# A fourteenth slot in the big SBUF pool of a hybrid attention and gated delta rule step

## The chip, the cores and the metric

The kernel runs on one core of a Trainium2 chip, as one program and one launch. The metric is the device time of an execution in microseconds (us). Engines are named as in the profile: PE is TensorE's matmuls and PEld its weight loads, DVE is VectorE, ACT is ScalarE, POOL is GpSimd, SP is SyncE.

## The reference, cut to what matters

One layer of a decoder is run on a prompt of 256 tokens and on 8 sequences that each add one token to a past of 2048. Two mixers run side by side on one normalised input: sparse attention (compressed, selected and window branches) and a gated delta rule (a short causal convolution on q, k and v, then chunks of 64 tokens that carry a state of 128 x 128 per head). All arithmetic is in 32-bit floats.

```python
def decoder_layer(x_p, x_s, cache_cmp, cache_slc, st_win, st_S, st_conv, page_table, w):
    ...
    (q_a, kvc, kvs, kvw, g_nsa, z_a, qkv_b, a_b, b_b, z_b, gate_a, gate_b) = split_proj(rms_norm(x_p, norm_w) @ w_in)
    q, kvc, kvs, kvw = nsa_project(q_a, kvc, kvs, kvw, q_norm_w, k_norm_slc_w, k_norm_win_w)
    o_cmp, o_slc, o_win = nsa_prompt(q, kvc, kvs, kvw, cw, slopes)
    y_a = nsa_merge(o_cmp, o_slc, o_win, g_nsa, z_a, w_pa)
    y_b, S_p, conv_p = gdn_branch(qkv_b, a_b, b_b, z_b, zero_conv, zero_S, *gw)
    y_p = merge_residual(x_p, y_a, y_b, gate_a, gate_b, w_o)
    ...
def gdn_branch(qkv, a, b, z, conv_buf, S0, conv_w, a_log, dt_bias, gdn_norm_w, w_pb):
    buf = jnp.concatenate([conv_buf.astype(qkv.dtype), qkv], axis=1)
    c = jax.nn.silu(causal_conv(buf, conv_w)).astype(jnp.float32)
    ...
    o, S = gdn_chunked(q, k, v, g, beta, S0.astype(jnp.float32))
    ...
    return o @ w_pb, S.astype(S0.dtype), buf[:, -(CONV_W - 1):]
```

The outputs are the new rows of both inputs, the rows for all caches, the window buffers, and the states of the delta rule and of the convolution. `gdn_chunked` solves one triangular system of 64 x 64 per head and chunk.

## The kernel before, in words

**Matmuls.** Prompt and decode rows lie side by side as 264 columns (`TT`, 256 + 8). Each product of 32-bit matrices is made of three faster ones: a weight is split into `hi` (rounded, by ACT, L332) and `lo` (the rest, by DVE, L333), the input likewise into `xh` and `xl`, and `three` (its matmuls run through the helper line L205) adds `xh` x `hi`, `xl` x `hi` and `xh` x `lo` in PSUM. A unit of 1024 x 128 weights is a *half*: 8 blocks, 24 matmuls of 264 columns.

**The loop.** The list `halves` holds all halves in the order of the projections (`ORDER`, L30): first those of the compress stage (`CQ`: pages of the cache are loaded by `load_pages`, L386, by SP and POOL in turn, split at L409 and L410, and multiplied with `w1h` and `w1l`), then the projections of q, k, v and the gates, the two output projections, and the last one. For half i the loop loads the weights of half i + 4 (SP, L327), splits those of half i + 2, and issues the matmuls of half i in two parts. After each part `tick()` lets every running generator issue its next piece: `g_xnorm` (normalises the input; its squares are summed by the DVE reduction `xa`, L295), the attention's, `g_gdn` (prompt part of the delta rule), `g_gdn_dec` (its decode part, from L1361).

**Order.** SP's and POOL's instructions run in the order in which the program writes them. The order on PE, DVE and ACT is set at build time by a scheduler that simulates the engines, so a change of buffers can shift it.

**The big pool.** `slot()` takes a tile of 8448 B per partition from the pool `s8`, with `NS` = 13 buffers. Tiles take them in turn as they come free: cache pages, the input (`xt`), the split weights of the compress stage, q/k/v rows (`qkvr`), the tile `qm` (masked decode queries), the state tiles `sst`, the tiles of the delta rule (`At`, `U`, `prod`), and others. A tile that takes a used buffer waits for its last reader.

**The delta rule's prompt part.** POOL writes the diagonal 16 x 16 blocks of `At` to memory (`ad`, L1190) and reads them back one per lane into `prod` (L1197); DVE inverts them there in 15 steps (L1205, L1206), POOL scatters the inverses into `U` through memory (`td`, L1210 to L1216), and PE builds the inverse of the whole from them (`inv`).

**Its decode part.** Four state tiles `sst`, each for two sequences, are loaded by ACT (L1370), read by PE (`sw`), scaled (ACT, L1459) and added to (DVE, L1460), and stored by ACT (`o_Ss`, L1463); after each store the load of the tile after next is issued from the same queue. Before that, the old convolution rows `cd` (loaded by SP at L1058, 2304 B per partition) are written on to the output by POOL (L1374) and used by DVE (L1383). The decode temporaries `dsq`, `dx`, `dr`, `deb`, `wq`, `dod` and `dvn` are tiles of their own in the pool `tp`.

**The scratch.** The program reserves 8192 B for POOL's dynamic transfers (`dynamic_dma_scratch_size`, in `build`).

Of the kernel before, what the change touches and what calls it, by code (L numbers as in the profile page):

```python
# [20 lines left out]
NB = 8  # L21
# [123 lines left out]
def program(tc, A):  # L145
# [6 lines left out]
        ctxs.append(p)  # L152
        return p.__enter__()

    NS = 13
    cp = pool("cp")
    st = pool("st")
    s8 = pool("s8", bufs=NS)
# [10 lines left out]
    def slot(name, shape, dt=F32):  # L169
        return s8.tile(shape, dt, tag="s8", name=name)  # L170
# [68 lines left out]
    gd = cp.tile([128, 64], F32, name="gd")  # L239
    grow = cp.tile([128, 2], F32, name="grow")  # L240
    acc2 = cp.tile([128, 128], F32, name="acc2")
    cd = cp.tile([128, 24, 3, NB], F32, name="cd")
    cpo = cp.tile([128, 24, 3], F32, name="cpo")
    qss = cp.tile([128, 2, 8], F32, name="qss")
    beh = cp.tile([128, 2, 8], F32, name="beh")
# [255 lines left out]
    def g_qstat(h):  # L501
        yield
        pt = psb("qtr")
        jk = tp.tile([128, 128], F32, name="jk", tag="jk")
        for t in range(2):
            tr(pt[:, 128 * t:128 * t + 128], L["qT"][:, h, 128 * t:128 * t + 128])
        for t in range(2):
            S.activation(jk, pt[:, 128 * t:128 * t + 128], AF.Square, accum_out=ssq[:, t, h:h + 1])
        if h == 7:
            yield  # L510
            rsq(rqs, ssq, 1.0 / 128, EPS, [128, 2, 8])
            sl = C("slp").rearrange("p (t h) -> p t h", t=2)
            V.tensor_scalar(srq, ssq, 1.0 / 128, EPS, ALU.mult, ALU.add)
            V.tensor_mul(srq, srq, rqs)
            V.tensor_mul(srq, srq, sl)
            V.tensor_scalar(rqs, rqs, SCALE, None, ALU.mult)
            qr = L["qT"][:, :, TP:TT]
            sq = tp.tile([128, 8, NB], F32, name="qsq", tag="qsq")
            S.activation(sq, qr, AF.Square)
            yield 2  # L520
            p2 = psb("qss")
            mm(p2[:, 0:64], ones, sq.rearrange("p h b -> p (h b)"))
            rd = tp.tile([128, 64], F32, name="qrd", tag="qrd")
            rsq(rd, p2[:, 0:64], 1.0 / 128, EPS, [128, 64])
            o = qd.rearrange("p g b r -> p g r b")
            for g in range(2):
                V.scalar_tensor_tensor(o[:, g], qr[:, 4 * g:4 * g + 4, :], P("qw"),
                                       rd.rearrange("p (g r b) -> p g r b", g=2, r=4)[:, g], ALU.mult, ALU.mult)
            qx = slot("qm", [128, 640])
            G.memset(qx, 0.0)  # L530
            L["qdp"] = qdp = qx[:, 0:128]
            L["qm"] = qm = qx[:, 128:640].rearrange("p (j i c) -> p j i c", j=4, i=4)
            for bp in range(2):
                V.tensor_copy(qdp[:, 64 * bp:64 * bp + 64].rearrange("p (g c) -> p g c", g=2)[:, :, 0:16]
                              .rearrange("p g (i r) -> p g i r", r=4),
                              qd.rearrange("p g (i c) r -> p c g i r", c=2)[:, bp])
            for i in range(4):
                V.tensor_copy(qm[:, :, i, 4 * i:4 * i + 4],
                              qdp.rearrange("p (j c) -> p j c", j=4)[:, :, 4 * i:4 * i + 4])
            mark("q")  # L540
# [511 lines left out]
    def ev_qkv(j):  # L1052
        def f(ps):
            k, h = j // 8, j % 8
            if h == 0:
                L["qkv", k] = slot("qkvr", [128, 8, TT])
                if k == 0:
                    SP.dma_start(cd, A["cst8"])  # L1058
                if k == 1:
                    L["ktk"] = slot("ktk", [128, 2, 8, 128])  # L1060
                if k == 2:
                    L["vbt"] = slot("vbt", [128, 2, 8, 128])
# [301 lines left out]
    def g_gdn_dec():  # L1364
# [6 lines left out]

        state(0)
        state(2)
        G.dma_start(A["o_convs"][:, :, 0:2, :], cd[:, :, 1:3, :])  # L1374
        cw = P("cw").rearrange("p (j i) -> p j i", i=4)
        cv = tp.tile([128, 24, NB], F32, name="dcv", tag="a", bufs=NA)
# [8 lines left out]
        mark("gnew")  # L1385
        S.activation(th, cv, AF.Tanh, scale=0.5)
        V.scalar_tensor_tensor(cv, th, 1.0, cv, ALU.add, ALU.mult)
        sq = tp.tile([128, 16, NB], F32, name="dsq", tag="dsq", bufs=2)
        S.activation(sq, cv[:, 0:16], AF.Square)
        x = tp.tile([72, 2, 64], F32, name="dx", tag="dsq", bufs=2)  # L1390
        V.memset(x, 0.0)
        eg8 = tp.tile([128, NB], F32, name="eg8", tag="eg8")
        S.activation(eg8[32:40], sm[32:40, TP:TT], AF.Exp)
# [6 lines left out]
        pt = PGD("dg")  # L1400
        mm(pt[:, 0:128], ones, sq.rearrange("p h b -> p (h b)"))
        mm(pt[:, 128:256], ones[0:72, :], x.rearrange("p a c -> p (a c)"))
        r = tp.tile([128, 128], F32, name="dr", tag="dsq", bufs=2)
        rsq(r, pt[:, 0:128], 1.0, 4 * EPS, [128, 128])
        eb = tp.tile([128, 2, 64], F32, name="deb", tag="deb")
        S.activation(eb, pt[:, 128:256].rearrange("p (a c) -> p a c", a=2), AF.Copy)
        f64 = lambda a: a.rearrange("p h b -> p (h b)")
        qk = cv[:, 0:16]
        V.scalar_tensor_tensor(f64(cv[:, 0:8]), f64(cv[:, 0:8]), SCALE, r[:, 0:64], ALU.mult, ALU.mult)
        V.tensor_mul(f64(cv[:, 8:16]), f64(cv[:, 8:16]), r[:, 64:128])  # L1410
        q, k, v = f64(cv[:, 0:8]), f64(cv[:, 8:16]), f64(cv[:, 16:24])
        wq = tp.tile([128, 80, 2], F32, name="wq", tag="wq")
        V.memset(wq[:, 64:80], 0.0)
        u = tp.tile([128, 64], F32, name="du", tag="dcp")
        kq = tp.tile([128, 64], F32, name="dkq", tag="qsq")
# [6 lines left out]
        p2 = PGD("dq")  # L1422
        mm(p2[:, 0:64], ones, kq)
        V.tensor_copy(kq, p2[:, 0:64])
        od = tp.tile([128, 64], F32, name="dod", tag="dod")
        vn = tp.tile([128, 64], F32, name="dvn", tag="dvn")
        hb3 = lambda a: a.rearrange("p (h b) -> p h b", h=8)
        yield 2
        for b0 in range(0, NB, 2):
# [270 lines left out]


def build(m):
    nc = _bacc.Bacc("TRN2", target_bir_lowering=False, num_devices=1, dynamic_dma_scratch_size=8192)
    A = {}
    for k, a in m.items():
        A[k] = nc.dram_tensor(k, a.shape, mybir.dt.from_np(a.dtype), kind="ExternalInput").ap()
# [35 lines left out]
```

## Time and profile before

| what | value |
|---|---|
| median of 3 runs | 1135.54 us (1135.36 to 1137.25) |
| the profiled execution | 1137.88 us |
| its span, first to last instruction | 1136.2 us |
| its mean granted clock of TensorE | 0.994 of full speed |
| PE busy | 1112.4 us, 98% of the span, 9558 matmuls |
| PEld busy | 1069.3 us, 94% |
| DVE busy | 697.1 us, 61% |
| ACT busy | 572.7 us, 50% |
| POOL busy | 144.2 us, 13% |
| DMA | 222.17 MB, 196 GB/s in the mean |

The busy shares are means over the whole execution. Matmuls are pipelined and their ends are modelled, so PE's spacing, from the start of one matmul to the start of the next, says more than its busy time. Idle time of an engine that is not the bottleneck costs nothing. What one profiled execution shows is compared with its own time, 1137.88 us, and only then with the median.

### The profile page before, as it was taken

Reading aid. Unit: us, or ns where it says so; the run is one execution under the profiler, and the core shown is the slowest. Engines: PE = TensorE matmul, PEld = TensorE weight load, DVE = VectorE, ACT = ScalarE, POOL = GpSimd, SP = SyncE. Lnnn points to the kernel's source line nnn. Section 1 sums busy time; section 2 is a strip of 40 time slices with the busy share of each in tenths; the row PEclk is TensorE's granted clock in tenths of the full one; section 3 lists DMA queues with packets and bytes.
Section 4 is the critical chain, followed back from the end, with each engine's and each line's share of the span. In section 5 each row is a group of like instructions: output and inputs, shape, how many; then the busy total and the mean of one; then the engine's idle time right before and its main releaser. Section 6 shows DMA issues by size and latency. Waiting matters only on the chain.

```text
span 1136.2 us, 25323 instructions
## 1 busy us (share of the span) xinstructions
PE 1112.4 (98%) x9558; PEld 1069.3 (94%) x9558; DVE 697.1 (61%) x1523; ACT 572.7 (50%) x1138; POOL 144.2 (13%) x227
## 2 busy tenths in 40 slices
PE   4999999999999999999999999999999999999998
PEld 3989999999999987897989999999999999999998
DVE  3578565443657776783566577677547575487443
ACT  4445655444634766673454465545344554444332
POOL 4430244200001310113022100102000000000000
PEclk9989999999999999999999899999999999999999
DMA  9873676435445784568998755657454355556663
GB/s 302 255 241 124 202 205 203 152 95 160 161 138 177 218 214 135 159 196 220 281 390 291 268 174 176 201 179 220 138 187 148 119 165 177 181 184 223 201 236 125
DMA packets 77069, 222.17 MB, mean 196 GB/s; under 512 B 10625, under 2 KB 27850, under 8 KB 75410
## 3 DMA queue, kind: packets, MB, share of 16 engines
q1 hardware_dynamic: 59346, 164.36, 44.7%
q0 software_dynamic: 15008, 44.98, 13.8%
q10 hardware_dynamic: 2592, 11.21, 2.6%
q8 instruction: 75, 1.23, 0.4%
q14 instruction: 48, 0.39, 0.1%
HBM read 202.90 MB, written 17.60 MB: 194 GB/s over the span
## 4 chain that ended last, share of the span: by engine, by line
PE 92%; DVE 1%; ACT 0%; issue 0%; ACTq 0%
PE acc L205 77%; PE inv L205 1%; PE po L205 1%; PE gtr L202 1%; PE pvo L205 1%; PE ps L205 1%; PE gsc L205 1%; PE cf L205 1%; PE kk L205 1%; PE vnb L202 1%; PE uw L205 1%; DVE xt L306 1%; PE pst L202 0%; PE og L205 0%; PE wsc L205 0%; PE kvtr L202 0%
## 5 line engine op out<-in xcount | busy, mean ns | idle before, releaser
L333 DVE TENSOR_TENSOR lo<-raw,hi 128x1024 fp32r<-128x1024 f32 (+1 forms) x250 | 304.8, 1220 | 212.5 <-ACT hi L332 206.1
L205 PE MATMUL acc<-xh,hi 128*128 128x264 f32 (+1 forms) x1488 | 433.8, 292 | 0.0
L332 ACT ACTIVATE hi<-raw 128x1024 fp32r<-128x1024 f32 (+1 forms) x250 | 263.9, 1056 | 329.7 <-PE acc L205 269.0
L205 PE MATMUL acc<-xl,hi 128*128 128x264 f32 (+1 forms) x1488 | 426.9, 287 | 0.5 <-issue 0.5
L205 PE MATMUL acc<-xh,lo 128*128 128x264 f32 (+1 forms) x1488 | 426.3, 287 | 0.0
L205 PEld LDWEIGHTS acc<-xh,hi 128*128 128x128 f32 (+1 forms) x1488 | 281.0, 189 | 7.6 <-issue 7.0
L205 PEld LDWEIGHTS acc<-xh,lo 128*128 128x128 f32 (+1 forms) x1488 | 280.0, 188 | 2.7 <-issue 2.2
L205 PEld LDWEIGHTS acc<-xl,hi 128*128 128x128 f32 (+1 forms) x1488 | 281.1, 189 | 1.5 <-issue 1.0
L205 PE MATMUL acc<-hi,w1h 128*128 128x254 f32 (+1 forms) x512 | 148.1, 290 | 15.9 <-ACT hi L409 15.9
L205 PE MATMUL acc<-lo,w1h 128*128 128x254 f32 (+1 forms) x512 | 147.4, 288 | 3.4 <-DVE lo L410 3.2
L205 PE MATMUL acc<-hi,w1l 128*128 128x254 f32 (+1 forms) x512 | 145.7, 285 | 0.0
L410 DVE TENSOR_TENSOR lo<-rawc,hi 128x512 fp32r<-128x512 f32 (+2 forms) x136 | 84.0, 656 | 52.5 <-ACT hi L409 48.1
L205 PEld LDWEIGHTS acc<-hi,w1h 128*128 128x128 f32 x512 | 98.4, 192 | 16.0 <-ACT hi L409 15.9
L409 ACT ACTIVATE hi<-rawc 128x512 fp32r<-128x512 f32 (+2 forms) x136 | 74.7, 599 | 62.7 <-PE acc L205 58.0
L205 PEld LDWEIGHTS acc<-lo,w1h 128*128 128x128 f32 x512 | 99.2, 194 | 4.8 <-DVE lo L410 4.5
L205 PEld LDWEIGHTS acc<-hi,w1l 128*128 128x128 f32 x512 | 99.0, 193 | 0.1
L386 POOL DMA_DIRECT2D rawc<-ccmp x125 | 67.3, 538 | 98.2 <-issue 72.3
L205 PE MATMUL acc<-oh,hi 128*128 128x264 f32 x256 | 73.5, 287 | 0.0
L205 PE MATMUL acc<-oh,lo 128*128 128x264 f32 x256 | 72.9, 285 | 0.0
L205 PE MATMUL acc<-ol,hi 128*128 128x264 f32 x256 | 72.7, 284 | 0.0
L205 PE MATMUL acc<-mh,hi 128*128 128x264 f32 x256 | 72.6, 284 | 0.0
L205 PE MATMUL acc<-ml,hi 128*128 128x264 f32 x256 | 72.5, 283 | 0.0
(452 smaller groups left out, 1476.4 us busy)
## 6 DMA issues: line engine op xcount, KB each, us to landing
raw<-win SPq DMA_DIRECT2D x184, 512.0 KB, 3.5
raw<-wpab SPq DMA_DIRECT2D x32, 512.0 KB, 3.9
raw<-wo SPq DMA_DIRECT2D x32, 512.0 KB, 4.3
rawc<-ccmp SPq DMA_DIRECT2D x126, 128.0 KB, 2.7
rawc<-ccmp POOLq DMA_DIRECT2D x125, 128.0 KB, 3.3
raw<-w SPq DMA_DIRECT2D x8, 512.0 KB, 7.6
wk<-winK SPq DMA_DIRECT2D x8, 512.0 KB, 11.1
o_wk<-wk POOLq DMA_DIRECT2D x8, 512.0 KB, 9.0
```

The lines of the kernel that those rows point to most:

```text
L202: T.transpose(out, in_, ident[0:n, 0:n])
L205: T.matmul(out, lhsT, rhs, start=start, stop=stop, **k)
L306: V.scalar_tensor_tensor(xt[i][:, k, :], xt[i][:, k, :], P("nw")[:, kk:kk + 1], rx, ALU.mult, ALU.mult)
L332: S.activation(self.hi, self.raw, AF.Copy)
L333: V.tensor_sub(self.lo, self.raw, self.hi)
L386: e.dma_start(rawc[kv, b][j // 8][:, j % 8].rearrange("p s c g -> p (s c g)"), src[kv, bass.ds(r, 1)].rearrange("o d f -> (o d) f"))
L409: S.activation(h, src, AF.Copy)
L410: V.tensor_sub(l, src, h)
```

## The change

`NS` goes from 13 to 14, and the room for the 8448 B of the new slot is made in three places:

- The convolution rows `cd` are no longer a tile of their own. They take columns 640 to 1216 of `qm`, whose tile grows from 640 to 1216 columns in the slot it has anyway. POOL still clears only the first 640.
- The seven decode temporaries become parts of two tiles `za` and `zb` of 384 columns, of the tag `zz`, which the softmax of the attention uses (2 buffers).
- The scratch for dynamic transfers is halved, from 8192 to 4096 B.

```diff
-    NS = 13
+    NS = 14
...
-    cd = cp.tile([128, 24, 3, NB], F32, name="cd")
...
-            qx = slot("qm", [128, 640])
-            G.memset(qx, 0.0)
+            qx = slot("qm", [128, 1216])
+            G.memset(qx[:, 0:640], 0.0)
+            L["cd"] = qx[:, 640:1216].rearrange("p (j i b) -> p j i b", j=24, i=3)
...
-                    SP.dma_start(cd, A["cst8"])
+                    SP.dma_start(L["cd"], A["cst8"])
...
         state(0)
         state(2)
+        za, zb = (tp.tile([128, 384], F32, name=n, tag="zz", bufs=2) for n in ("dga", "dgb"))
+        cd = L.pop("cd")
...
-        sq = tp.tile([128, 16, NB], F32, name="dsq", tag="dsq", bufs=2)
+        sq = zb[:, 0:128].rearrange("p (h b) -> p h b", b=NB)
...
-        x = tp.tile([72, 2, 64], F32, name="dx", tag="dsq", bufs=2)
+        x = zb[0:72, 128:256].rearrange("p (a c) -> p a c", a=2)
...
-        r = tp.tile([128, 128], F32, name="dr", tag="dsq", bufs=2)
+        r = zb[:, 0:128]
...
-        eb = tp.tile([128, 2, 64], F32, name="deb", tag="deb")
+        eb = za[:, 0:128].rearrange("p (a c) -> p a c", a=2)
...
-        wq = tp.tile([128, 80, 2], F32, name="wq", tag="wq")
+        wq = za[:, 128:288].rearrange("p (c w) -> p c w", w=2)
...
-        od = tp.tile([128, 64], F32, name="dod", tag="dod")
-        vn = tp.tile([128, 64], F32, name="dvn", tag="dvn")
+        od, vn = za[:, 288:352], zb[:, 256:320]
...
-    nc = _bacc.Bacc("TRN2", target_bir_lowering=False, num_devices=1, dynamic_dma_scratch_size=8192)
+    nc = _bacc.Bacc("TRN2", target_bir_lowering=False, num_devices=1, dynamic_dma_scratch_size=4096)
```

Source lines behind L526 move by one or two. SP and POOL keep their order. On PE, DVE and ACT the scheduler arranges some instructions in another way; three places follow.

DVE where the inversion of the 16 x 16 blocks begins (`zt` and `ol` belong to the gated attention output, `lo` to a weight of the projections, `prod` to the inversion). Before:

```order
L1490 SCALAR_TENSOR_TENSOR zt<-zt,acc 128x264
L1491 SCALAR_TENSOR_TENSOR zt<-zt,qT 128x264
L1198 MEMSET prod 128x256
L1201 MEMSET prod 128x512
L1199 MEMSET prod 128x16
L333 TENSOR_TENSOR lo<-raw,hi 128x1024
L1493 TENSOR_TENSOR ol<-zt,oh 128x264
L1205 TENSOR_TENSOR prod<-prod 128x1
```

And in the change:

```order
L1494 TENSOR_TENSOR ol<-zt,oh 128x264
L332 TENSOR_TENSOR lo<-raw,hi 128x1024
L1491 SCALAR_TENSOR_TENSOR zt<-zt,acc 128x264
L1492 SCALAR_TENSOR_TENSOR zt<-zt,qT 128x264
L1205 TENSOR_TENSOR prod<-prod 128x1
L1206 TENSOR_REDUCE prod<-prod 128x1
L1205 TENSOR_TENSOR prod<-prod 128x4
```

The first step of the inversion stands behind a `zt` three units of the output gate earlier, the one that ran at 738.43 us before, and the clearing of `prod` has moved further ahead.

ACT around the second store of a state tile, with what each entry waits for (`DMA..` is a transfer's landing, `hi` a weight's split, `gate` a sigmoid of the output gates; the scaling factor is `deb` before and `dga` in the change). Before:

```order
L332 ACTIVATE hi<-raw 128x1024 [waits DMAHW1_49,DVE_49,PE_49]
L1504 ACTIVATE gate<-acc 128x264 [waits PE_49]
L1463 DMA o_Ss<-sst 128x2048 [waits DVE_49]
L332 ACTIVATE hi<-raw 128x1024 [waits DMAHW2_49,PE_49,Activation_49]
L1459 ACTIVATE sst<-sst,deb 128x128 [waits PE_49] x5
```

And in the change:

```order
L1464 DMA o_Ss<-sst 128x2048 [waits DVE_49]
L331 ACTIVATE hi<-raw 128x1024 [waits DMAHW1_49,PE_49,Activation_49]
L1505 ACTIVATE gate<-acc 128x264 [waits PE_49]
L331 ACTIVATE hi<-raw 128x1024 [waits DMAHW2_49,PE_49,Activation_49]
L1460 ACTIVATE sst<-sst,dga 128x128 [waits PE_49] x6
L1370 DMA sst<-stS 128x2048 [waits DMAHW3_49]
L1460 ACTIVATE sst<-sst,dga 128x128 [waits PE_49]
```

The load of the fourth state tile now stands five entries behind the store and waits for its landing. Before, that load came much later, at 839.1 us.

PE at the first matmuls of the inverse. Before they stand in a half of the gates' projections, which multiplies `xh` and `xl`:

```order
L205 MATMUL acc<-xh,hi 128x264
L205 MATMUL acc<-xl,hi 128x264
L205 MATMUL inv<-U,At 128x64 x8
L205 MATMUL acc<-xh,lo 128x264
L205 MATMUL acc<-xh,hi 128x264
```

In the change they stand in the last matmuls of a half of the first output projection, which multiplies `oh` and `ol`:

```order
L205 MATMUL acc<-oh,hi 128x264
L205 MATMUL acc<-ol,hi 128x264
L205 MATMUL acc<-oh,lo 128x264
L205 MATMUL acc<-oh,hi 128x264
L205 MATMUL inv<-U,At 128x64 x8
L205 MATMUL acc<-ol,hi 128x264
L205 MATMUL acc<-oh,lo 128x264
L205 MATMUL acc<-xh,hi 128x264
```

The inverse has moved by 162 entries of PE's order towards the start, about 20 us of matmuls, and stays among them.

## Rows read from the trace of the kernel before

**Rows 1.** The page, busy time, share of the span and instructions.

```profile
PE 1112.4 (98%) x9558; PEld 1069.3 (94%) x9558; DVE 697.1 (61%) x1523; ACT 572.7 (50%) x1138; POOL 144.2 (13%) x227
```

**Rows 2.** What PE waited for: us in total, times, longest (us).

```profile
PE acc L205 <- ACT hi L409: 15.9, 1, 15.9
PE acc L205 <- DVE lo L410: 3.2, 2, 2.6
...
PE acc L205 <- issue: 0.5, 1, 0.5
```

**Rows 3.** The chain that ended last: start (us), length (us), what.

```profile
537.64 3.01 PE acc L205 x24
...
705.76 5.80 PE acc L205 x48
```

**Rows 4.** Timeline of DVE: start, us, what, [idle before, releaser].

```profile
67.20 4.14 DVE L295 TENSOR_REDUCE xa<-xsq 128x264 f32<-128x2112 f32 x1 [0.85 <-ACT xsq L294]
```

**Rows 5.** Windows: us, PE, PEld, DVE, ACT, POOL busy (instructions), PEclk, DMA, GB/s.

```profile
72.00:76.00 4.00, 3.41 (x16) 3.41 (x17) 3.62 (x7) 0.00 (x0) 1.78 (x4) 0.50 0.86 251
76.00:80.00 4.00, 4.00 (x23) 3.79 (x23) 1.53 (x5) 1.15 (x2) 1.08 (x2) 0.65 1.00 336
...
636.00:640.00 4.00, 4.00 (x19) 4.00 (x20) 1.90 (x7) 1.49 (x3) 0.00 (x0) 0.50 1.03 350
640.00:644.00 4.00, 4.00 (x27) 4.00 (x27) 0.00 (x0) 0.00 (x0) 0.00 (x0) 0.75 0.56 185
...
500.00:550.00 50.00, 49.49 (x514) 41.78 (x516) 24.19 (x57) 23.87 (x45) 11.88 (x12) 1.00 0.85 224
```

**Rows 6.** Timeline of PE, narrow matmuls of the decode part.

```profile
634.62 1.36 PE L205 MATMUL dec<-smt,cst 128*128 128x8 f32 x8
```

**Rows 7.** What SP's queue waited for, 100 to 215 us.

```profile
SPq L386 <- DVE lo L410: 18.3, 5, 8.1
```

**Rows 8.** Timeline of POOL, the delta rule's transfers.

```profile
724.22 4.49 POOL L1190 DMA_DIRECT2D ad<-At  x8 [94.01 <-DVE At L1180]
757.44 0.57 POOL L1197 DMA_DIRECT2D prod<-ad  x1 [28.74 <-DVE zt L1491]
...
794.02 0.56 POOL L1213 DMA_DIRECT2D U<-td  x1
```

**Rows 9.** Timeline of DVE, first step and closing copy of the inversion.

```profile
760.56 0.16 DVE L1205 TENSOR_TENSOR prod<-prod 128x1 f32<-128x1 f32 x1 [0.99 <-DMA prod<-ad]
...
782.38 0.38 DVE L1209 COPY prod<-prod 128x256 f32<-128x256 f32 x1
```

**Rows 10.** The tile U, 785 to 800 us: its eight transfers, issue to landing.

```profile
DMA to landing us min/median/max: 5.7/5.7/5.7
```

**Rows 11.** Timeline of ACT around the stores of the first two state tiles.

```profile
688.55 0.36 ACTq L1463 DMA_DIRECT2D o_Ss<-sst  x1
...
695.70 0.37 ACT L1504 ACTIVATE gate<-acc 128x264 f32<-128x264 f32 x1
...
766.22 0.35 ACTq L1463 DMA_DIRECT2D o_Ss<-sst  x1
...
769.92 1.56 ACT L1459 ACTIVATE sst<-sst,deb 128x128 f32<-128x128 f32 x5
772.61 1.06 ACT L332 ACTIVATE hi<-raw 128x1024 fp32r<-128x1024 f32 x1 [1.13 <-issue]
```

**Rows 12.** Timeline of PE around the first matmuls of the inverse.

```profile
804.51 1.90 PE L205 MATMUL inv<-U,At 128*128 128x64 f32 x16
806.22 0.37 PE L205 MATMUL acc<-xh,lo 128*128 128x264 f32 x1
806.42 0.28 PE L205 MATMUL acc<-xh,hi 128*128 128x264 f32 x1
```

**Rows 13.** Groups by line: busy us, mean ns | idle before, releasers.

```profile
L333 DVE TENSOR_TENSOR lo<-raw,hi 128x1024 fp32r<-128x1024 f32 (+1 forms) x250 | 304.8, 1220 | 212.5 <-ACT hi L332 206.1 <-PE acc L205 2.1 <-PE inv L205 2.0
```

**Rows 14.** The state tiles sst, their loads' issue to landing.

```profile
DMA to landing us min/median/max: 6.7/9.2/11.7
```

## The prediction

> **What bounds the kernel now.** The page's busy table comes first: TensorE's matmuls fill 1112.4 of 1136.2 us [rows 1]. A busy share alone doesn't prove that an engine sets the end, so the second view is the list of what PE waited for. It has four rows for the whole execution, from 15.9 us, the first operand's arrival at the start, over 3.2 us down to 0.5 [rows 2]. No row names a DMA. The third view is the chain of work that ended last: it runs along PE, and in its long pieces the 264-column matmuls follow each other every 0.121 us (48 in 5.80) in one place and every 0.125 us (24 in 3.01) in the stretch that mixes them with attention [rows 3]. So from about 20 us on the time is the number of matmuls, each at its own pace, plus two scars:
>
> - At 69.8 us PE waits 2.6 us for `lo` [rows 2]. VectorE has a 4.14 us reduction of the input's squares in front of that `lo` [rows 4]. In the two stretches of 4 us behind the wait TensorE's granted clock is 0.50 of full speed (2.4 GHz) and 0.65 [rows 5], which are 2.0 + 1.4 = 3.4 us lost at most, about 3 if the part in which PE waited is taken off.
> - At 634.6 us come eight-column matmuls [rows 6], and behind them the clock is 0.50 and 0.75 for 4 us each (19 and 27 matmuls instead of 33) [rows 5]. That is (14 + 6) x 0.121 = 2.4 us, with a little before 636: about 2.8.
>
> What the change can give back is therefore small from the outset: 2.6 + 3 + 2.8 = 8.4 us plus whatever the start yields.
>
> **The change part by part.**
>
> *The fourteenth slot.* Tiles of the big pool are allocated in the same order, and each now waits for the release of one tile further back. The waits that this shortens stand on the loading queues: SP waits 18.3 us in five pieces for `lo` of the compress stage to free a page slot [rows 7]. PE never waits for a page in that time [rows 2], so these 18.3 us are worth nothing on the path. Nor does the slot touch the two scars: the reduction at 67.20 waits 0.85 us for ScalarE, not for a slot [rows 4], and the order of VectorE, ScalarE and PE is unchanged around both places. Value: 0. Should the 0.85 go, it is 0.85 and a share of the slow clock, under 2 us.
>
> *The chain of the gated delta rule.* `prod` no longer inherits the slot of a tile that VectorE's `zt` must finish with. Before, POOL wrote the diagonal blocks to memory at 724.22 to 728.71 and then stood 28.74 us until `zt` released the slot [rows 8]; now it may read them back as soon as they have landed. With 5.7 us, the landing of the similar scatter into `U` [rows 10], that issue falls at 734.4, and with the 3.1 us that the same load took before (757.44 to 760.56, the last 0.99 of them waited for by VectorE) [rows 8, 9] its data are there at about 737.5. In the new order VectorE's first `prod` stands right behind the `zt` that ran at about 738.4 before, so about 22 us earlier than 760.56, and a wait there is nought to 2 us. What queues behind it is `lo`. A `lo` is made two halves ahead of its use: two halves of PE last 2 x 24 x 0.121 = 5.8 us, `hi` takes 1.06 and `lo` 1.22 [rows 3, 11, 13], so 3.5 us of delay stay hidden. Value: 0. The inverse on PE moves forward with it. Before, the chain's copy ended at 782.76, the last `U` scatter was issued at 794.02 and landed 5.7 us later, at 799.7, and PE came to the inverse at 804.51 [rows 8 to 10, 12]: 4.8 us to spare. The new order keeps the distance from copy to inverse at about 22 us, so the margin stays. Nothing of this shortens PE's list, since the inverse is squeezed between matmuls of the projections either way, and the later half of the inverse and what follows stand where they stood. Value: 0, not the 22 us by which the chain starts earlier.
>
> *More switches on PE.* By the new order PE changes between kinds of matmul ten times more often. Going into the inverse cost nothing, and leaving it 0.20 instead of 0.121 us (806.22 to 806.42) [rows 12]. If only every second switch costs, that is 5 x 0.08 = 0.4 us, and if each does, 0.8. I take +0.5.
>
> *Decode temporaries in two softmax tiles.* The same instructions on the same engines, with other addresses. ScalarE's order moves around the state tiles, though. The fourth load of the state stands, in the new order, five entries behind the store of the second one, and must wait until that store has landed, since it takes its slot; on ScalarE's queue everything behind it waits too. The store was issued at 766.22, and the new place comes behind six scalings of the state, of which five ended at 771.48 before, so at about 771.9, 5.7 us later [rows 11]. How long a store takes to land no row says directly. From below: at 695.70 an instruction that needed the first store (issued 688.55) ran without waiting, so that one took at most 7.15 us [rows 11]. From above: the slowest load of such a tile took 11.7 us [rows 14]. I take the row that is the same kind of transfer: at most 7.15, a wait of 0 to 1.5 us, with 3.5 us of cover. Value: 0. At 11.7 it is 6 us of wait, 2.5 of them on PE, and a slow clock after it.
>
> *Conv state in the `qm` slot.* One SP load and three VectorE reads at another address; POOL clears the same 640 columns. The slot is held longer, which the fourteenth one pays for. Value: 0.
>
> *Half the scratch.* The scratch holds descriptors of POOL's transfers. The trace shows no row of POOL waiting for it; bound from above: POOL blocks until earlier transfers are done. Where its transfers are finely divided, before 630 us, POOL has nothing to do afterwards until 724.22 (idle 94.01) [rows 8], which hides any such wait; in the page loads an issue may be late by a landing time, against 18.3 us that the queues waited anyway [rows 7]. Value: 0.
>
> **Sum.** Profiled execution: 1137.88 (span 1136.2 and 1.7 around it) + 0.5 = 1138.4. This execution was 2.3 above the median of the runs, so against 1135.54 it is **1136.0 us**: no change. A measurement of this kernel can tell about 0.2% (2.3 us) from no change.
>
> **Rivals.**
>
> 1. *Faster: a scar vanishes.* What decides the clock behind the eight-column matmuls is not in the rows, and its neighbours are shifted by fractions of a microsecond. Without that scar: 1136.0 - 2.8 = 1133.2. Against it: the same matmuls in the same order. If the stall at 69.8 goes with its slow clock, 1136.0 - 5.6 = 1130.4; against it, VectorE's order is the same. Chance 0.08 together.
>
> 2. *Faster: the middle is starved of work, and the slot feeds it.* In 500 to 550 us the weight loads are busy 41.78 of 50 us while the matmuls show 49.49 [rows 5]. If that gap were idle time that waits for slots, up to 8.2 us would come back there: 1127.8. Against it: the spacing there is 0.125, against 0.121 elsewhere [rows 3], so at most 514 x 0.0045 = 2.3 us, and PE's list of waits names no load. The weight loads are sparse there because each of many matmuls is wide. Chance 0.02. The Trainium skill ("Perfetto Trace Analysis", Identifying the Most-Contended Engine) says that matmul busy share is no good measure of the distance to the roofline and that the busy share of weight loads is; read so, this stretch is the place with room. The trace disagrees on what that room is, by the spacing.
>
> 3. *Slower: ScalarE stands at the state load.* If the second store lands as late as the slowest state load, 11.7 us, ScalarE is held until 777.9, `hi` of 772.61 comes 6 us late, and PE runs dry for 2.5 us; a stall of 2.6 us cost some 3 us of slow clock on top (rows of 69.8 us). 1136.0 + 5.5 = 1141.5. It decides from a landing of about 5.7 + 3.5 = 9.2 us on. For it: landings of 9 and more occur among the loads. Against it: the first store's 7.15. Chance 0.08.
>
> 4. *Slower: the earlier delta chain meets a late transfer.* If the read-back of `ad` lands over 5 us after VectorE reaches it, or `U` more than 4.8 us later than before, PE or VectorE stands in order. A stall of 1 us and the clock's 3: 1140. Chance 0.04.
>
> 5. *The change does not do what it says*, for the slots or the scratch bind nowhere: that is my forecast's own case on the clock, and gives the same 1136.0.
>
> **How the numbers follow.** Forecast 0.78, its own range 1133.7 to 1137.8 (runs of before span 1135.36 to 1137.25, switches 0 to +0.8). Faster by over 0.2%: 0.08 + 0.02 = 0.10. Slower: 0.08 + 0.04 = 0.12. To leave no more than 2 in 10 outside, the range takes in the first rival's nearer half and the beginning of the slower ones: 1133.2 to 1138.8.
>
> **What would show it.** In the changed kernel PE's waits should be the same rows, 15.9 and two of `lo`, and no new ones; the chain's pieces keep 0.121. SP's wait for `lo` shrinks and nothing else follows. The first `prod` runs near 739 and the inverse near 784, with the same end. ScalarE's row behind the state load near 772 shows how long the store took. I am wrong if PE has a new wait between 730 and 800, or if a row of the granted clock differs at 72 to 80 or 636 to 644.

## The result: slower by 0.5 to 0.7%

The changed kernel takes 1144.27 us (median of 6 runs, 1141.12 to 1147.02) against 1137.04 for the kernel before, measured beside it: ratio 1.0067, 95% interval 1.0055 to 1.0079. In a second measurement (again, 5 runs) it was 1139.79 against 1135.17, ratio 1.0051 (1.0038 to 1.0064). The forecast was 1136.0 in a range up to 1138.8, so both lie outside. The profiled execution took 1144.40 us, its span is 1142.4 (the page of the changed kernel):

```profile
span 1142.4 us, 25297 instructions
...
PE 1114.6 (98%) x9558; PEld 1069.8 (94%) x9558; DVE 697.4 (61%) x1523; ACT 573.0 (50%) x1138; POOL 145.4 (13%) x227
```

As many matmuls and nearly the same busy shares as in [rows 1]. What PE waited for in the changed kernel (us in total, times, longest):

```profile
PE acc L205 <- ACT hi L408: 17.9, 3, 14.1
PE acc L205 <- DVE lo L409: 3.8, 3, 2.6
PE acc L205 <- issue: 2.0, 2, 1.0
PE pvo L205 <- ACT wP L798: 0.6, 1, 0.6
```

Against [rows 2] there are two more waits for `hi` besides the first operand's (1.5 and 2.3 us), one more for `lo`, and 2.0 us for which the profile names nothing (`issue`; the kernel before has 0.5). The windows of the changed kernel show where PE stood or ran slowly (us, busy time of PE, PEld, DVE, ACT, POOL with instructions, granted clock, DMA share, GB/s):

```profile
28.00:32.00 4.00, 4.00 (x24) 4.00 (x23) 2.60 (x6) 0.23 (x1) 2.11 (x4) 0.58 0.84 243
72.00:76.00 4.00, 2.09 (x17) 2.09 (x18) 4.00 (x8) 0.55 (x2) 1.62 (x3) 1.00 1.02 364
76.00:80.00 4.00, 4.00 (x34) 3.94 (x33) 3.69 (x10) 1.16 (x2) 0.54 (x1) 1.00 0.55 179
132.00:136.00 4.00, 1.54 (x10) 1.12 (x9) 1.34 (x3) 2.95 (x7) 1.40 (x4) 1.00 0.55 163
536.00:540.00 4.00, 3.53 (x17) 3.52 (x17) 0.49 (x1) 1.36 (x2) 0.00 (x0) 0.57 1.03 222
...
640.00:644.00 4.00, 4.00 (x19) 4.00 (x20) 1.76 (x7) 1.27 (x2) 0.00 (x0) 0.50 0.99 390
```

The clock fell behind other stalls than in [rows 5]: not after the wait at 70 us (1.00 in both windows, against 0.50 and 0.65), but at 28 and at 536 us. Part of this differs from execution to execution: the second trace of the changed kernel (again) has 1.00 at 28 and at 536 us. The slow clock behind 70 us goes mostly with the number of slots. In the window from 72 to 76 us it is 0.50 to 0.70 in all four traces with thirteen slots and the 4.14 us reduction of [rows 4], and below 1.00 in one of the eight with fourteen (hold_w1, 0.60), though PE's wait of about 2.6 us ahead of it is in all twelve. Why is open.

Yet the total of the clock does not explain the loss: the mean granted clock of the changed kernel's runs is 0.9948 in the first measurement and 0.9954 in the second, that of the kernel before 0.9958 there. Counted without it (span times mean clock, averaged over the runs), the second still has 1132.7 against 1128.9, so about 3.8 us come from waits and from matmuls that follow each other less closely.

Where the time goes shows when the k-th matmul of the changed kernel's trace is set beside the k-th of the kernel before. The changed kernel is 1.5 us ahead at 130 us, since it runs at the full clock behind 70 us, and 1.5 us behind at 140. It is still 1.4 us behind at 500, then 4.6 at 560, of which 1.7 us are the slow clock there. Between 700 and 900 us it loses 1.8 us more and stays 6.4 us behind to the end. So there are three places: 132 us, 530 to 545 us, and the stretch from 645 to 850 us.

**The wait at 132 us.** PE's first matmul after the gap, and on ACT what stood ahead of its `hi` (timelines of the changed kernel, PE and ACT):

```profile
134.57 0.40 PE L205 MATMUL acc<-hi,w1h 128*128 128x286 f32 x1 [2.27 <-ACT hi L408]
```

```profile
133.05 1.06 ACT L366 ACTIVATE w1h<-raw 128x1024 fp32r<-128x1024 f32 x1 [2.63 <-DMA raw<-w]
134.01 0.92 ACT L408 ACTIVATE hi<-rawc 128x384 fp32r<-128x384 f32 x2
```

In the kernel before, this split of compress weights ran at 140.49 us. Its load was also issued later. SP's timeline of the kernel before, and then of the changed one:

```profile
116.32 14.60 SPq L386 DMA_DIRECT2D rawc<-ccmp  x6
130.96 0.43 SPq L357 DMA_DIRECT2D raw<-w  x1
...
133.89 0.43 SPq L357 DMA_DIRECT2D raw<-w  x1
```

```profile
121.54 0.37 SPq L356 DMA_DIRECT2D raw<-w  x1
125.32 1.47 SPq L385 DMA_DIRECT2D rawc<-ccmp  x2
126.84 1.17 SPq L356 DMA_DIRECT2D raw<-w  x1
```

**The stretch from 645 to 850 us.** The tile view gives the first and the last start of the matmuls `sw` of the decode part, which stand at the same places among the 264-column matmuls in both orders. The kernel before, then the changed one:

```profile
L205 PE MATMUL sw<-sst,wq x128: 272/273/297, 660.9 to 848.4; 128*32 128x128 f32 x128
```

```profile
L205 PE MATMUL sw<-sst,dga x128: 272/273/298, 665.5 to 854.8; 128*32 128x128 f32 x128
```

187.5 us became 189.3, at full clock and without a wait that the profile lists.

### The profile page after: what moved, and what is told of

It is laid out like the page before. It is cut to its first block, busy times and chain, and to the rows that moved or that the text cites. A ratio compares the mean times of both kernels' runs of the same rounds, so it can differ in the third digit from the quotient of the medians.

```text
span 1142.4 us, 25297 instructions
## 1 busy us (share of the span) xinstructions
PE 1114.6 (98%) x9558; PEld 1069.8 (94%) x9558; DVE 697.4 (61%) x1523; ACT 573.0 (50%) x1138; POOL 145.4 (13%) x227
## 4 chain that ended last, share of the span: by engine, by line
PE 91%; DVE 1%; issue 0%; SPq 0%; ACT 0%; DMA 0%; ACTq 0%
PE acc L205 75%; PE inv L205 1%; PE po L205 1%; PE gtr L202 1%; PE pvo L205 1%; PE ps L205 1%; PE gsc L205 1%; PE cf L205 1%; PE kk L205 1%; PE uw L205 1%; PE vnb L202 1%; DVE xt L305 1%; PE pst L202 0%; PE og L205 0%; PE sw L205 0%
## 5 line engine op out<-in xcount | busy, mean ns | idle before, releaser
L205 PEld LDWEIGHTS acc<-hi,w1h 128*128 128x128 f32 x512 | 97.9, 191 | 18.4 <-ACT hi L408 18.3
```

What stands on the lines that cost most here:

```text
L205: T.matmul(out, lhsT, rhs, start=start, stop=stop, **k)
```

## The experiments

Each ratio is to the kernel before, measured beside it, with its 95% interval. A trace is that of a single execution, which can be faster or slower than the median: the traced executions of again and hold_from_q were the fastest of their runs (1137.2 us against a median of 1139.8, and 1134.8 against 1140.9).

**Which part?** The three other parts of the change without the slot, and the smallest of them alone.

```diff
# slots13: the changed kernel
-    NS = 14
+    NS = 13
# scratch_half: the kernel before
-    nc = _bacc.Bacc("TRN2", target_bir_lowering=False, num_devices=1, dynamic_dma_scratch_size=8192)
+    nc = _bacc.Bacc("TRN2", target_bir_lowering=False, num_devices=1, dynamic_dma_scratch_size=4096)
```

> The changed kernel with thirteen slots: half the scratch, the decode temporaries in the softmax tiles and the convolution rows in the shared slot stay. Theory A: the slot is the cause, so the time is that of the kernel before, 1136 to 1138.5. Theory B (scratch): 1140 to 1144, nearly the changed kernel. Theory C: 1137 to 1139, since PE's order is close to that of the kernel before (16 rows differ in place of 74).

> The kernel before with only the scratch halved, 4096 B; the order on all engines is the same. Theories A and C: no change, 1136 to 1138.5. Theory B (the smaller scratch shifts POOL's first loads, so that PE starts earlier, runs dry at 24 us and is clocked down): 1139 to 1141, with PE waits for hi and lo at 24 to 26 us.

slots13: 1135.54 us, ratio 0.9999 (0.9987 to 1.0010). scratch_half: 1135.51 us, 1.0008 (0.9999 to 1.0017). The loss is the fourteenth slot's. scratch_half did show waits at 24 to 26 us and a clock of 0.65 at 28, in the order of the kernel before, and its time is that of the kernel before: an earlier first matmul (13.4 us) runs into loads that come no sooner.

The changed kernel once more, for a second trace:

> The changed kernel once more, unaltered, for a second trace. Theory A: again about 2.3 us of PE wait at 132 us behind the split that waits for raw<-w, and 1142 to 1146. Theory B: again a first matmul at about 14 us, 1.5 and 1.0 us of PE wait at 24 to 26 us and a clock under 0.9 behind it. If the waits at 24 or 534 us are chance, they differ here and the time of the single runs spreads by several us.

Ratio 1.0051 (1.0038 to 1.0064). PE waits again at 131 us (1.3 us, and 0.2), and 2.0 us are lost between 130 and 140 us; `sw` again spans 189.3 us. The 2.0 us without a name at 535 us are not there, and nothing is lost between 500 and 560 us in this trace, which is that of the fastest run.

**Is it the split that stands ahead on ACT?** hold_w1 gives the splits of two weight tiles a scale of 1.0 that DVE writes only at a later place, so that ACT's queue has them where they stood before.

```diff
# hold_w1: the changed kernel
+    one = cp.tile([128, 1], F32, name="one")
...
-            S.activation(h, self.raw, AF.Copy)
+            S.activation(h, self.raw, AF.Copy, scale=one if kv == 1 and q > 1 else 1.0)
...
+            if (kv, b, s0) == (0, 7, 11):
+                V.tensor_scalar(one, self.lo[:, 0, 0:1].bitcast(F32), 0.0, 1.0, ALU.mult, ALU.add)
```

> The changed kernel, but the last two splits of the compress weights (w1h on ScalarE, third and fourth of the v half) take a scale of 1.0 from a value that VectorE writes late, so that they stand at about 139 us as in the kernel before, not at 126 and 133. Theory A (these two splits, moved ahead by the fourteenth slot, wait for their load in front of a split that PE needs: 2.3 us of PE wait at 132 us, at times with a slow clock behind it): the wait at 132 is gone and the time falls from 1144.3 by 2.4 to 5 us, to 1139.5 to 1142. Theory B (the start and the halved scratch): no effect at 132 matters, 1144 stays. Theory C (PE's new order between 500 and 850 us costs it): 1142 to 1144, since PE's order is that of the changed kernel.

1138.99 us, ratio 1.0034 (1.0020 to 1.0048); counted without the clock 1132.7, no less than again. The split no longer stands ahead (it runs at 145.0 us), and PE still waits at 134 us, 1.5 us and 0.2. ACT's timeline of hold_w1, and the landing of two page loads that POOL issued at 129.1 and 130.3 us, the third and fourth behind its store `o_kvc` (min, median, max):

```profile
135.60 0.94 ACT L409 ACTIVATE hi<-rawc 128x384 fp32r<-128x384 f32 x2 [2.79 <-issue]
```

```profile
DMA to landing us min/median/max: 5.0/5.1/5.2
```

The second of the two landed at 135.53 us, and the `hi` that PE lacks starts at 135.60. The same two pages in slots13, which has thirteen slots and no wait there, issued at 127.3 and 128.5 us, and then three later pages of slots13, issued from 132.3 to 134.9 us:

```profile
DMA to landing us min/median/max: 2.5/2.7/2.8
```

```profile
DMA to landing us min/median/max: 4.9/5.1/5.4
```

So theory A fell: with the split out of the way ACT waits for the page itself. Slow landings are not new with the slot; slots13 has them as well. What moved is where they fall. SP issues its two loads of 512 KB at 123.8 and 129.4 us in hold_w1, and at 129.7 and 132.6 in slots13. In both kernels the page loads that took about 5 us were issued beside the second of these loads or in the 2.3 us behind it. With fourteen slots SP's six page loads ahead of them take 6.3 us in place of 14.6, so the 512 KB go out 7 to 9 us earlier than in the kernel before, and the slow landings meet the pages that PE needs next. POOL comes to these pages late in every kernel: the store `o_kvc` stands ahead of them and waits for its data, 42 us in the kernel before, 46 in the changed one, 49 in hold_w1. In the changed kernel itself the page and the split of the weights were ready at nearly the same time (about 133.8 and 134.0 us), so taking the split away could help little.

**Do the early loads delay the pages?** w1_late is hold_w1 with both weight loads two pages later in SP's order, and store_act lets POOL fetch its pages early:

```diff
# w1_late: hold_w1, and
-             (0, 7, 2): [(1, 0), (1, 1)], (1, 0, 0): [(1, 2), (1, 3)]}
+             (0, 7, 2): [(1, 0), (1, 1)], (1, 0, 1): [(1, 2), (1, 3)]}
# store_act: the changed kernel
-                G.dma_start(A["o_kvc"], L["kvc"])
+                S.dma_start(A["o_kvc"], L["kvc"])
```

> The changed kernel, with the two splits of compress weights held as before (hold_w1), and with their loads placed one piece of the compress stage later in SP's order, behind two more page loads. hold_w1 still had 1.7 us of PE wait at 134 us, on page data. Theory D (the fourteenth slot lets SP issue these two loads of 512 KB some 7 us earlier, and they delay the pages that PE needs first): no PE wait between 125 and 145 us, and the time is that of the kernel before plus about 1.5 us that all three traces with fourteen slots show between 645 and 850 us, a ratio of 1.0005 to 1.002. Rival A (it is the split on ScalarE alone): as hold_w1, 1.0034. Rival E (the wait has to do with the slots of the pages, not with these loads): the PE wait at 132 to 135 us stays above 1 us.

> The changed kernel, but the store o_kvc is issued by ScalarE and not by POOL, whose page loads stood behind it for 46 us (until 122.7). SP's early loads stay. Theory D: POOL's pages are fetched well ahead of need, so nothing is late at 131 to 135 us and PE does not wait there; ratio to the kernel before 1.000 to 1.002. Rival A: one split of the compress weights still stands on ScalarE ahead of its load, so 1 to 2.5 us of PE wait stay at 132 us; ratio 1.003 to 1.006.

w1_late: 1138.23 us, ratio 1.0021 (1.0008 to 1.0033). store_act: 1138.17 us, 1.0022 (1.0011 to 1.0034). What PE waited for in store_act (w1_late has the same rows, with the waits of 24 us beside them):

```profile
PE acc L205 <- ACT hi L408: 15.1, 1, 15.1
PE acc L205 <- DVE lo L409: 3.6, 2, 2.6
PE pvo L205 <- ACT wP L798: 0.6, 1, 0.6
```

There is no wait of more than 0.2 us around 132 us in either; between 130 and 140 us w1_late still loses 0.8 us and store_act nothing. POOL's timeline of store_act shows page loads at 100 to 104 us that came at 124 and later in the changed kernel:

```profile
100.24 0.54 POOL L385 DMA_DIRECT2D rawc<-ccmp  x1 [4.43 <-DVE xl L310]
...
104.38 0.54 POOL L385 DMA_DIRECT2D rawc<-ccmp  x1 [0.66 <-issue]
```

So both ways of parting the loads from the pages take the wait away, and more than half of the loss is gone in the times, as theory D (the early loads delay the pages) had it. w1_late is not a sure cure: tree_w1_late below waits 1.2 us and 0.2 at 131 again. A last step in this direction, both loads behind all the pages in question:

```diff
# w1_later: hold_w1, and
-             (0, 7, 2): [(1, 0), (1, 1)], (1, 0, 0): [(1, 2), (1, 3)]}
+             (0, 7, 2): [(1, 0), (1, 1)], (1, 0, 2): [(1, 2), (1, 3)]}
```

> w1_late moved on: the two loads of compress weights come ten page loads behind the second one and directly after each other in SP's order, two pieces later than in the changed kernel; the splits stay held. In tree_w1_late the pages still landed late (up to 5.3 us) and PE waited 1.4 us at 131. Theory D: with the loads behind the pages, the pages between 126 and 136 us land in 2.4 to 3.2 us as in the kernel before, there is no PE wait at 131 to 135, and the ratio is that of the switches alone, 1.001 to 1.002. Rival E (the pages are late by POOL's blocked queue whatever the loads do): a PE wait of over 1 us and ratio 1.003 as in hold_w1. If the weights now come too late themselves, a PE wait for w1h or w1l appears at 145 to 155 us.

Ratio 1.0046 (1.0032 to 1.0060), a miss: its trace has no wait at 131 to 135 us and is yet slow, so the page wait is not all that the slot costs. Against the kernel before, its trace loses 0.8 us between 130 and 140 us, 1.6 between 500 and 560, and 1.75 at the switches of kind (below). It has this row among PE's waits:

```profile
PE acc L205 <- issue: 1.9, 2, 1.0
```

These waits end at 533 and 534 us; those of the changed kernel end at 535 and 536. Around there POOL's gathers of values had moved too, in all kernels that have fourteen slots at that time: two gathers that went at 522 us now stand 9.6 us and head a burst. POOL's timeline of the changed kernel:

```profile
528.04 0.97 POOL L891 DMA_INDIRECT gv<-cslv,idx  x1 [9.62 <-issue]
529.32 0.96 POOL L891 DMA_INDIRECT gv<-cslv,idx  x1 [0.30 <-issue]
530.59 0.97 POOL L891 DMA_INDIRECT gv<-cslv,idx  x1 [0.30 <-PE cvt L205]
```

**The switches alone.** `prod` out of the pool, so that its chain starts early with thirteen slots:

```diff
# prod_own: slots13, and
-        prod = slot("prod", [128, 1536])
+        prod = cp.tile([128, 1536], F32, name="prod")
```

> Thirteen slots with all other parts of the change (slots13), and the tile prod taken out of the pool into space of its own, so that the chain of the delta rule starts early as with fourteen slots while the compress stage stays as before. By the order, PE changes between kinds of matmul ten times more often, as in the changed kernel. Theory C' (this early chain costs 1.5 us between 645 and 850 us, by the switches, with no wait): PE's matmuls arrive 1.3 to 1.8 us later over this stretch, no PE wait at 131 to 135 us, ratio 1.001 to 1.0018. Rival (the 1.5 us come from the slots in that stretch, not from the order): the stretch takes as long as in the kernel before, ratio 1.000.

1138.30 us, ratio 1.0016 (1.0004 to 1.0028). The tile view of prod_own, and of slots13, whose chain starts late:

```profile
L205 PE MATMUL sw<-sst,dga x128: 272/273/298, 659.8 to 849.1; 128*32 128x128 f32 x128
```

```profile
L205 PE MATMUL sw<-sst,dga x128: 272/273/298, 659.0 to 846.6; 128*32 128x128 f32 x128
```

189.3 and 187.6 us: the early chain gives the whole 1.75 us, with thirteen slots too. Summed over the starts of PE's matmuls between the first and the last `sw` (1870 in both, of the same kinds), the gaps within one kind take 0.24 us less and the gaps between kinds 1.99 us more, 93 of them in place of 83. That is 0.18 us for each further switch.

**The burst, and the rest of the slot.** A tile that nobody needs takes one slot at the q projections (hold_from_q) or at the kvc projections (hold_from_kvc) and keeps it to the end:

```diff
# hold_from_q: the changed kernel, in ev_q (hold_from_kvc: in ev_kvc)
             if j == 0:
+                L["dum"] = slot("dum", [128, 1])
+                V.memset(L["dum"], 0.0)
...
+    at_end(lambda: V.tensor_copy(acc2[:, 0:1], L["dum"]))
```

> The changed kernel, but a tile that nobody needs takes one slot when the q projections begin and keeps it to the end, so that thirteen are left from there on; in the order POOL's gathers of values wait for the same tiles as in the kernel before, and the delta chain stays early. Theory F (the fourteenth slot makes the gathers wait for a tile that lives longer, they go out in a burst at 526 to 531 us, and PE's instructions come late in it): gathers in pairs from 520 us on, no unnamed PE wait over 0.8 us at 525 to 536; what is left is the page wait at 132 us (1.4 to 2.4) and the switches (1.75): ratio 1.0025 to 1.0045. Rival (the burst costs nothing): ratio as the changed kernel, 1.005 to 1.0067.

> The same with the tile taken when the kvc projections begin (about 100 us), so before the pages that were late at 132 us are fetched. Theory D, F and C' together: no PE wait at 131 to 135 us, none over 0.8 us at 525 to 536, the delta chain early: the switches alone, ratio 1.001 to 1.002 as prod_own (1.0016). If something else of the fourteenth slot costs time (before 100 us, or the mere address of the tiles): 1.003 or more.

hold_from_q: 1140.89 us, ratio 1.0041 (1.0026 to 1.0056), single runs from 1134.8 to 1145.0. hold_from_kvc: 1138.19 us, 1.0015 (1.0005 to 1.0025). In both the gathers start at 519 us again. hold_from_kvc has no wait at 132:

```profile
PE acc L205 <- ACT hi L408: 15.1, 2, 14.8
PE acc L205 <- DVE lo L409: 3.6, 2, 2.6
PE pvo L205 <- ACT wP L800: 0.6, 1, 0.6
PE acc L205 <- issue: 0.3, 1, 0.3
```

It stands where prod_own stands, at the switches alone. So what the slot costs beyond them in these two kernels comes from what it does between the kvc projections (from about 105 us) and the q projections (from about 250 us): 1.0041 against 1.0015, with intervals that just do not meet. The traces differ there in one place only, from 130 to 140 us, where the page wait lies: hold_from_q loses 1.5 us and hold_from_kvc 0.3. That is less than the 3 us between the medians; but the trace of hold_from_q is that of its fastest run, and what its slower runs lost no trace shows.

That the burst at 528 us costs time is not shown: without it the ratio is 1.0041, with it 1.0051 and 1.0067, and 1.0041 and 1.0051 overlap. PE's waits without a name between 527 and 536 us hint at it. Of the eight traces with the burst three have 1.8 to 2.0 us of them (the changed kernel, w1_later, tree_store_act) and five none; the eight traces without it have 0.7 us at most. It stays open, and with it what makes w1_later slow.

**What is a wait of PE worth?** The wait at 70 us is in both kernels. It was taken away by another way of summing:

```diff
# tree: the kernel before
-            V.tensor_reduce(a2[i], sq.rearrange("p k t -> p t k"), AX.X, ALU.add)
+            V.tensor_add(sq[:, 0:4], sq[:, 0:4], sq[:, 4:8])
+            V.tensor_add(sq[:, 0:2], sq[:, 0:2], sq[:, 2:4])
+            V.tensor_add(a2[i], sq[:, 0], sq[:, 1])
# tree_x_early: tree, and in g_xnorm ahead of the loads of xt
-        yield 30
+        yield 24
```

> The kernel before, but the squares of the input are summed by three additions of halves (128x1056, 528, 264) in place of each reduction of 4.14 us. It prices a PE wait: at 70 us PE waits 2.6 us in every trace so far, and the clock falls behind it in four of six. If a wait of PE is paid in full, the time falls by 2.6 to 5 us: ratio 0.9955 to 0.9977. If the gap is taken back later, 1.000.

> w1_late and tree together, on the changed kernel. If the two act apart: the ratio of w1_late less what tree gains, 0.996 to 0.9995. If with fourteen slots a PE wait at 132 us takes the place of the one at 70, 1.000 to 1.003.

> The kernel before with tree's additions, and the load of the input started six ticks (about 8 us) earlier, since in tree the gain at 70 us was given back at 92 to 100 us, where the normalised input came too late. If that was the only obstacle: 2.6 to 6 us gained, ratio 0.995 to 0.998. If the pages are now late, since the input holds three slots earlier: 1.000 or more.

> The changed kernel with the store o_kvc on ScalarE, tree's additions and the input's load six ticks earlier: no PE wait at 70 and at 132 us, and the fourteenth slot covers the input's earlier tiles. Theory D with C': the gain of tree in full less the 1.5 us of the early delta chain, ratio 0.996 to 0.9995. If PE's wait only moves on: 1.001 to 1.003.

tree: 1134.90 us, ratio 0.9993 (0.9983 to 1.0003), no change. The wait at 70 is gone, and with it the slow clock behind it. PE's matmuls that ran at 79 to 96 us in the kernel before come about 6.4 us earlier; those of 100 to 104 us are only about 2.7 us earlier. PE's timeline of tree and its window:

```profile
93.62 0.39 PE L205 MATMUL acc<-xh,hi 128*128 128x264 f32 x1 [1.91 <-ACT hi L334]
```

```profile
92.00:96.00 4.00, 2.33 (x10) 2.13 (x11) 4.00 (x6) 2.54 (x4) 0.00 (x0) 0.74 0.61 197
```

PE came to the projections before the normalised input was there. With the input's load 5.4 us earlier (44.0 us against 49.4 in tree), tree_x_early: **1131.62 us, ratio 0.9958 (0.9945 to 0.9972)**, faster than both kernels. What PE waited for in it:

```profile
PE acc L205 <- ACT hi L411: 16.1, 1, 16.1
PE acc L205 <- DVE lo L412: 1.3, 2, 1.0
PE pvo L205 <- ACT wP L800: 0.6, 1, 0.6
PE acc L205 <- issue: 0.4, 1, 0.4
```

On the changed kernel the gain is used up: tree_store_act, which has the earlier input load too, has 1.0009 (0.9997 to 1.0022). In its trace PE is 5.5 us ahead of the kernel before at 500 us, 3.8 at 560, behind 1.8 us of waits without a name, and 2.0 from 900 us on, behind the switches. tree_w1_late, which has tree's sum without the earlier input load, has 1.0014 (1.0005 to 1.0023).

## Why the prediction was wrong, point by point

**The slot's value, 0: the step that failed.** That PE never waits for a page was right of [rows 2], and the waits of SP's queue [rows 7] were indeed off the path. They shrank as forecast: SP's wait for `lo` between 100 and 215 us went from 18.3 us to 2.7. The mistake was to conclude that nothing else follows. A queue that runs ahead starts its next transfers earlier, here two loads of 512 KB, 7 to 9 us earlier, and the pages issued beside such a load took about 5 us to land where the same pages took 2.5 to 2.8 (hold_w1 and slots13). PE then waited 1.3 to 2.3 us at 132 us. The margin behind it was never worked out, neither POOL's late start behind `o_kvc` nor the cover of these pages. The prediction compared the order only around the two scars and at 700 to 850 us, and missed the two splits that moved ahead on ACT; that turned out not to be the cause by itself (hold_w1). What lies between hold_from_q and hold_from_kvc is about 0.26% or 3 us; the traces show 1.2 us (hold_from_q against hold_from_kvc) to 3.0 (the changed kernel) of it at this place. The 3.2 us that the changed kernel's trace loses between 500 and 560 us are missing in others, and their cause is open.

**"One tile further back" is not always earlier.** The two gathers went 5 us later with fourteen slots (POOL's rows at 528 us, behind w1_later above), and with one slot taken away again they went at 519 us (hold_from_q). That the tile further back lives longer there is read from the order of the instructions and shown by no row. That the delay costs time is open.

**The switches, +0.5 us: right mechanism, wrong size.** Measured 1.75 us. [rows 12] show one entry into the inverse, read as free, and one exit at 0.08 us above the pace; the sum needed the other switches too. In the kernel before, from one matmul's start to the next, the trace has on average 0.18 us into the inverse (12 switches), 0.13 out of it to a 264-column matmul (9), and 0.21 into and 0.20 out of `sw` (5 each), against 0.04 within the inverse, 0.03 within `sw` and 0.12 within the 264-column matmuls.

**The delta chain: right.** POOL's read-back, DVE's first step and the inverse in the changed kernel (timelines of POOL, DVE and PE), where everything stands 4.7 us later than before by then:

```profile
738.76 0.57 POOL L1197 DMA_DIRECT2D prod<-ad  x1 [5.42 <-issue]
```

```profile
743.41 0.15 DVE L1205 TENSOR_TENSOR prod<-prod 128x1 f32<-128x1 f32 x1
```

```profile
790.33 1.89 PE L205 MATMUL inv<-U,At 128*128 128x64 f32 x16
```

DVE waits for nothing there, PE neither, and the gain of 20 us in the chain is worth nothing, as said.

**The state load: right.** ACT's timeline of the changed kernel:

```profile
769.25 0.35 ACTq L1464 DMA_DIRECT2D o_Ss<-sst  x1
...
774.67 1.06 ACT L331 ACTIVATE hi<-raw 128x1024 fp32r<-128x1024 f32 x1 [1.33 <-issue]
775.59 0.33 ACTq L1370 DMA_DIRECT2D sst<-stS  x1
```

The load is issued as the `hi` ahead of it ends, 6.3 us behind the store, so the store had landed by then; rival 3 needed 9.2.

**Scratch, decode temporaries, conv state, 0 each: right** (scratch_half 1.0008, slots13 0.9999). The worst case by which the scratch was bounded, that POOL stands until earlier transfers are done, no run shows.

**The scars.** Rival 1 asked whether one would vanish. The prediction's own sign, another clock at 72 to 80 us, came true: with fourteen slots the slow clock behind 70 us is gone in seven of eight traces, although PE's stall there stayed at about 2.6 us. The gain did not last, since in the changed kernel's trace two other slow stretches took its place. Such a stretch taken singly is no measure of a change; the mean clock of all runs hardly moved.

**The other rivals.** Rival 2, the starved middle: the slot fed nothing there (the changed kernel lost 3.2 us between 500 and 560 us), and the weight loads' share, by which the Trainium skill ("Perfetto Trace Analysis", Identifying the Most-Contended Engine) judges the room, stayed at 94% of the span while the time rose. Rivals 3 and 4 forecast a loss of the right size at places where none arose; the page wait at 132 us was in a stretch for which I had no rival. Chances of 0.10, 0.78 and 0.12 were too sure for a kernel whose PE is busy 98% of the span: a new wait anywhere in its order can lengthen it, and the rivals covered only a few places.

## What to carry to other kernels

Where a buffer is added, list every transfer that may now start earlier and ask which needed transfer it will run beside, above all one that another queue issues late. Landing times mean something only for the same transfers in both kernels. Compare the order on every engine over the whole program, not only around the known stalls, and price a switch of kinds on TensorE from all kinds of switches. A wait that is removed from a busy engine pays only when the next producer is ready earlier as well, as tree and tree_x_early show.

## What the runs showed of the hardware that was not expected

Ten more switches between kinds of matmul, among the same 1870 matmuls and with the clock at its upper level, cost 1.75 us (prod_own against slots13). The stretch from the first to the last `sw` takes 189.3 us in the changed kernel, again, hold_w1, w1_late, w1_later, store_act, prod_own, hold_from_q, hold_from_kvc and tree_store_act and 189.5 in tree_w1_late, all with the early chain; it takes 187.5 and 187.6 in the kernel before and slots13.

PE's waits without a named releaser at 527 to 536 us range from none to 2.0 us between traces, also between the two traces of the changed kernel itself. They lie in a stretch with a DMA share of 0.98 to 1.05, but traces without such a wait have 1.00 to 1.05 there too. What PE lacks there no view shows, and it was not tried out.
